# Gate and up: two of eight K tiles by a 2x2 block product with seven products

## The chip, the cores and the metric
The kernel runs on one core of one Trainium2 chip. The metric is the device time of one launch in microseconds (us). The engines are TensorE (PE; its weight loads are PEld), VectorE (DVE), ScalarE (ACT), GpSimd (POOL) and SyncE (SP, which here only issues DMAs).

## The reference
One layer of a hybrid encoder in float32, for 256 rows (S) of width 2048 (D), with a feed-forward width of 5632 (DFF). The part that the change touches is the feed-forward half and the final norm:

```
x = x + concat([hg_out, sb_out, mla_out]) @ w_o
h = rmsnorm(x, ffn_norm_g)
x = x + (silu(h @ w_gate) * (h @ w_up)) @ w_down
out = rmsnorm(x, final_norm_g)
```
w_gate and w_up are 2048 x 5632, w_down is 5632 x 2048. Ahead of it stand an RMSNorm, one input projection and three mixers (a gated linear recurrence, stick-breaking attention and latent attention), which the change leaves alone.

## The kernel before
**Products.** Every large product runs as three float32r matmuls. A tile is split into a part that float32r holds (`hi`, a ScalarE cast) and the rest (`lo`, a VectorE subtraction), and hi*hi + hi*lo + lo*hi is summed in one PSUM bank. The split of weights is in `split_w`: SP loads a raw slab of 256 rows by 512 columns (512 KB, [128, 2, 512] on the chip) into one of four `raw` slots, ScalarE casts it into one of four `hi` slots (L119), VectorE subtracts into one of four `lo` slots (through the helper at L91). `gemm_mm` (L151 to L153) then issues 12 matmuls of 512 columns for a slab: two blocks of 128 rows of x (b), two halves of the slab (j), three products. The stationary operand comes from x, already transposed and split (`at` tiles from the pool actp, 16 slots of 4 KB per partition; [128, hi/lo, j, 256]); the moving operand is the slab.

**Order.** The program is written in order and a planner (the Tile framework's list scheduler) fixes each engine's order before the run: of what is ready it takes what has the best priority, and priority follows the order of the text. The weight split stands in `tc.high_priority(offset=400)` (AHEAD), so it counts as 400 instructions earlier than where it is written. At run time each engine's queue is in order; a slot of a pool is reused when its last reader is done. Small side tasks (transposes of a finished tile, for example) are generators: `spawn` puts one in a list, and `tick`, called after each slab, runs one step of the first two.

**PSUM.** Eight banks: psA has four (`acc_tile` takes two, one for each block of rows), psM four (`bank`, for transposes and small products).

**Output projection.** Four groups of 512 columns of w_o, eight slabs each. `wo_end` (L791) adds the result to x (tiles x2[0..3] in the slots R0 to R3), takes the squares for the norm on ScalarE, and spawns `turn_x2`: TensorE transposes, then ScalarE and VectorE (`split_act`, L156 and L94) write the hi and lo of the transposed x times the norm's gain into an `at` tile. Eight such tiles, x2T[0..7], each 256 rows of the contraction over D, are the K tiles of gate and up.

**Gate and up.** For each of 11 groups of 512 columns `ff` runs the eight slabs of w_gate, then those of w_up (L845 to L854). Each has its own pair of banks. Silu with the row norm r2 is a ScalarE pass out of PSUM (L849), the product with up a VectorE pass. `turn_hid` then transposes the 512 hidden columns during the next slabs (L246) and splits them out of PSUM: hidden tiles 0 to 7 into `at` slots, 8 to 21 into `ht` slots of the pool `late`.

**Down projection and end.** Four passes of 22 slabs of w_down over the 22 hidden tiles; `settle` adds a pass to x2, `finish_rows` scales the rows by the final norm and stores them. In the last pass the last four slabs are run for one block of rows and then for the other. The gain of the final norm is one tile `gf`, loaded once.

Of the kernel before, what the change touches and what calls it, by code (L numbers as in the profile page):

```python
# [26 lines left out]
G_ATTN, G_FFN, G_HG, G_SB, G_MLA, G_QN, G_KVN, G_END = 0, 16, 32, 36, 42, 48, 52, 54  # L27
# [24 lines left out]
WIDTH = 2  # L52
SABBUFS = 3
WARM = 9
MAGIC = 12582912.0
LOGEXP = "natural_log_exp_and_others"


def build(tc, x, xT, pos, gains, fgain, lbraw, w_in, w_uq, w_ukv, w_o, w_gate, w_up, w_down, cst, msk, out, dbg=None):
    nc = tc.nc  # L60
    pe, act, dve, pool, sp = nc.tensor, nc.scalar, nc.vector, nc.gpsimd, nc.sync
    dbg = dbg or {}
    es = ExitStack()
# [39 lines left out]
    ahead = [0]  # L103

    def split_w(w, r0, c0, n, pieces=1, between=None):
        raw = slabp.tile([P, 2, 512], F32, name=nm("raw"), tag="raw", bufs=4)
        with tc.high_priority(offset=ahead[0]):
            hi = slabp.tile([P, 2, 512], F32R, name=nm("hi"), tag="hi")
            lo = slabp.tile([P, 2, 512], F32R, name=nm("lo"), tag="lo")
            at = ROWS[w.tensor.name] * c0 + r0 * n  # L110
            wv = w[at:at + 2 * P * n].rearrange("(p t c) -> p t c", p=P, t=2)
            for j in range(pieces):
                js = slice(j * 2 // pieces, (j + 1) * 2 // pieces)
                if between and j:
                    between(j)
                sp.dma_start(raw[:, js, :n], wv[:, js, :])
            for j in range(pieces):
                js = slice(j * 2 // pieces, (j + 1) * 2 // pieces)
                act.copy(hi[:, js, :n], raw[:, js, :n])  # L119
                tt(lo[:, js, :n], raw[:, js, :n], hi[:, js, :n].bitcast(F32), ALU.subtract)  # L120
        return hi, lo

    def gemm_slab(acc, w, r0, c0, n, at, start, stop, pieces=1, between=None):
        gemm_mm(acc, split_w(w, r0, c0, n, pieces, between), n, at, start, stop)
        tick()

    tasks = []
    spawn = tasks.append

    def tick():  # L130
        for t in tasks[:WIDTH]:
            if next(t, tasks) is tasks:
                tasks.remove(t)
# [5 lines left out]
    def flush():  # L139
        while tasks:  # L140
            tick()
# [40 lines left out]
    def gc(base, i):  # L182
        return gcol[:, base + i:base + i + 1]
# [102 lines left out]
    def rt(i):  # L286
        return resid.tile([P, 2, 512], F32, name=nm("R"), tag=f"R{i}")
# [501 lines left out]
    late = es.enter_context(tc.tile_pool(name="late", bufs=2))  # L789

    def wo_end(a, g):  # L791
        t = x2[g]
        for b in range(2):
            tt(t[:, b, :], t[:, b, :], a[b], ALU.add)
            junk = late.tile([P, 512], F32, name=nm("junk"), tag="junk", bufs=1)
            act.activation(junk, t[:, b, :], AF.Square, accum_out=ss2[:, 2 * g + b:2 * g + b + 1])

        def turn_x2():
            yield
            for i in range(2):  # L800
                ps = transpose4([[t[:, b, (2 * i + j) * P:(2 * i + j + 1) * P] for b in range(2)] for j in range(2)])
                at = act_tile()
# [20 lines left out]
    r2 = rsqrt_mean(ssum, D, 2)  # L823


    hid = {}

    def ff(w, c0):
        a = acc_tile()
        for i in range(8):  # L830
            gemm_slab(a, w, i * 256, c0, 512, x2T[i], i == 0, i == 7)
        return a

    def turn_hid(g, hh):
        yield
        for i in range(2):
            ps = transpose4([[hh[:, b, (2 * i + j) * P:(2 * i + j + 1) * P] for b in range(2)] for j in range(2)])
            n = 2 * g + i
            at = act_tile() if n < 8 else late.tile([P, 2, 2, 256], F32R, name=nm("ht"), tag="ht", bufs=14)
            pv = ps.rearrange("p (j n) -> p j n", j=2)  # L840
            act.copy(at[:, 0, :, :], pv)
            tt(at[:, 1, :, :], pv, at[:, 0, :, :].bitcast(F32), ALU.subtract)
            hid[n] = at

    for g in range(11):  # L845
        a = ff(w_gate, g * 512)
        sg = late.tile([P, 2, 512], F32, name=nm("sg"), tag="sg", bufs=1)
        for b in range(2):
            act.activation(sg[:, b, :], a[b], AF.Silu, scale=r2[:, b:b + 1])  # L849
        a = ff(w_up, g * 512)  # L850
        hh = late.tile([P, 2, 512], F32, name=nm("hh"), tag="hh", bufs=1)
        for b in range(2):
            stt(hh[:, b, :], a[b], r2[:, b:b + 1], sg[:, b, :], ALU.mult, ALU.mult)
        spawn(turn_hid(g, hh))  # L854

    gf = late.tile([P, D], F32, name="gf", bufs=1)
    sp.dma_start(gf, fgain.partition_broadcast(P))
    ss3 = sm(10, "ss3", 1)

    def settle(g, b, a, cs, col):  # L860
        tb = x2[g][:, b, cs]
        tt(tb, tb, a[b][:, cs], ALU.add)
        junk = late.tile([P, 512], F32, name=nm("junk"), tag="junk", bufs=1)
        act.activation(junk[:, cs], tb, AF.Square, accum_out=ss3[:, 5 * b + col:5 * b + col + 1])

    def finish_rows(b, cols):
        ssum = sm(1)
        dve.tensor_reduce(ssum, ss3[:, 5 * b:5 * b + cols], axis=AX.X, op=ALU.add)
        r3 = rsqrt_mean(ssum, D, 1)
        for k in range(4):  # L870
            o = x2[k][:, b, :]
            if k in (0, 2):
                act.activation(o, o, AF.Copy, scale=r3)
            elif k == 3:
                stt(o, o, r3, gf[:, k * 512:], ALU.mult, ALU.mult)
            else:
                ts(o, o, r3, ALU.mult)
            sp.dma_start(out[b * P:(b + 1) * P, k * 512:(k + 1) * 512], o)

    whole, left, right = slice(0, 512), slice(0, 256), slice(256, 512)  # L880
    for g in range(4):
        a = acc_tile()
        held = 4 if g == 3 else 0
        for k in range(22 - held):
            gemm_slab(a, w_down, k * 256, g * 512, 512, hid[k], k == 0, k == 21)
        if not held:
            for b in range(2):
                settle(g, b, a, whole, g)
                tb = x2[g][:, b, :]
                tt(tb, tb, gf[:, g * 512:(g + 1) * 512], ALU.mult)  # L890
# [79 lines left out]
```

## Time and profile before
| what | value |
|---|---|
| median of 3 runs | 1147.61 us (1147.3 to 1148.05) |
| profiled execution, its own time | 1148.17 us |
| its span in the trace | 1146.4 us |
| output projection, last group ends near | 407 us |
| gate and up, then down projection | 407 to 898 us, 898 to 1133 us |
| granted TensorE clock, mean | 0.998 |
| HBM traffic | 207.94 MB read, 2.10 MB written |

The profile is of one execution. "Busy" is the share of the span in which an engine executes; matmuls are pipelined, so the row of one matmul is longer than the distance between two starts. "Idle before, releaser" is the time an engine stood still ahead of an instruction and who ended that. The difference between an execution's own time and its span lies outside what the trace covers.

### The profile page before, as it was taken

To read this page: it belongs to the slowest core of one execution; us is meant where nothing else is said; L and a number is where in the kernel's file an instruction comes from. 1 tells how busy PE (TensorE), PEld (TensorE's weight loads), DVE (VectorE), ACT (ScalarE), POOL (GpSimd) and SP (SyncE) were. 2 spreads that over 40 slices of the span, in tenths; PEclk is the share of its full clock that TensorE was granted. 3 is DMA by queue.
4 is the path that set the end of the run, shared out by engine and by line. 5 is a ranking of instruction groups with operands and counts; after the bars stand their busy time and mean duration, and the time that the engine had idled before them with its cause. 6 is when DMAs were issued, how large, how long until landed. Compare 5 with 4: busy or idle time off the path is not lost.

```text
span 1146.4 us, 14162 instructions
## 1 busy us (share of the span) xinstructions
PE 1132.0 (99%) x5429; PEld 955.0 (83%) x5429; DVE 618.7 (54%) x703; ACT 546.7 (48%) x712; POOL 76.4 (7%) x110
## 2 busy tenths in 40 slices
PE   8999999999999999999999999999999999999997
PEld 4888899999988888888888888888888888888886
DVE  7798565455556555454454454454554545454543
ACT  7665565566645454444444444444444434343433
POOL 3196000011100000000000000000000000000000
PEclk9999999999999999999999999999999999999999
DMA  7745465544765656566666666666665666666662
GB/s 260 242 144 168 126 180 176 155 132 140 220 211 181 189 191 188 190 191 189 189 190 191 188 189 191 186 189 193 187 198 184 185 191 194 185 194 190 186 195 97
DMA packets 72004, 210.97 MB, mean 184 GB/s; under 512 B 7296, under 2 KB 24448, under 8 KB 71808
## 3 DMA queue, kind: packets, MB, share of 16 engines
q1 hardware_dynamic: 71936, 210.07, 58.8%
q8 instruction: 42, 0.69, 0.2%
q14 instruction: 26, 0.21, 0.1%
HBM read 207.94 MB, written 2.10 MB: 183 GB/s over the span
## 4 chain that ended last, share of the span: by engine, by line
PE 94%; DMA 1%; issue 1%; DVE 1%; ACT 1%; POOL 0%; SPq 0%; ACTq 0%; POOLq 0%; DVEq 0%
PE acc L152 29%; PE acc L153 29%; PE acc L151 29%; PE bank L246 2%; DVE lo L91 1%; PE bank L710 1%; PE bank L409 1%; DMA raw<-w_in 1%; PE acc L588 1%; PE acc L587 1%; PE acc L586 0%; PE bank L709 0%; ACT hi L119 0%; DMA L<-xT 0%; DMA sA<-pos 0%
## 5 line engine op out<-in xcount | busy, mean ns | idle before, releaser
L91 DVE TENSOR_TENSOR lo<-raw,hi 128x1024 fp32r<-128x1024 f32 (+3 forms) x410 | 480.9, 1175 | 480.6 <-ACT hi L119 480.2
L119 ACT CAST hi<-raw 128x1024 fp32r<-128x1024 f32 (+3 forms) x410 | 408.3, 998 | 529.0 <-PE acc L153 516.8
L151 PE MATMUL acc<-hi,at 128*128 128x512 f32 (+2 forms) x1352 | 517.0, 384 | 0.4 <-ACT hi L119 0.4
L152 PE MATMUL acc<-lo,at 128*128 128x512 f32 (+2 forms) x1352 | 513.9, 380 | 3.0 <-DVE lo L91 2.9
L153 PE MATMUL acc<-hi,at 128*128 128x512 f32 (+2 forms) x1352 | 512.8, 380 | 0.0
L152 PEld LDWEIGHTS acc<-lo,at 128*128 128x128 f32 x1352 | 254.1, 188 | 49.9 <-DVE lo L91 7.5
L151 PEld LDWEIGHTS acc<-hi,at 128*128 128x128 f32 x1352 | 253.9, 188 | 45.7 <-ACT hi L119 2.0
L153 PEld LDWEIGHTS acc<-hi,at 128*128 128x128 f32 x1352 | 253.8, 188 | 43.3
L152 PE MATMUL acc<-lo,ht 128*128 128x512 f32 (+1 forms) x232 | 89.8, 387 | 0.0
L151 PE MATMUL acc<-hi,ht 128*128 128x512 f32 (+1 forms) x232 | 89.8, 387 | 0.0
L153 PE MATMUL acc<-hi,ht 128*128 128x512 f32 (+1 forms) x232 | 89.8, 387 | 0.0
L175 POOL TENSOR_TENSOR sm<-sm,expo 128x4 f32<-128x4 f32 (+2 forms) x14 | 12.0, 857 | 911.3 <-DVE sm L100 911.3
L152 PEld LDWEIGHTS acc<-lo,ht 128*128 128x128 f32 x232 | 43.5, 187 | 10.0
L153 PEld LDWEIGHTS acc<-hi,ht 128*128 128x128 f32 x232 | 43.5, 187 | 9.9
L151 PEld LDWEIGHTS acc<-hi,ht 128*128 128x128 f32 x232 | 43.5, 187 | 9.9
L156 ACT ACTIVATE at<-bank,gcol 128x256 fp32r<-128x256 f32 x38 | 16.7, 470 | 10.5 <-DVE at L94 10.5
L94 DVE SCALAR_TENSOR_TENSOR at<-bank,gcol,at 128x256 fp32r<-128x256 f32 x38 | 17.2, 478 | 4.0 <-ACT at L156 4.0
L849 ACT ACTIVATE sg<-acc,sm 128x512 f32<-128x512 f32 x22 | 15.1, 685 | 3.1 <-PE acc L153 3.1
L94 DVE SCALAR_TENSOR_TENSOR hh<-acc,sm,sg 128x512 f32<-128x512 f32 x22 | 15.4, 743 | 0.0
L160 POOL TENSOR_TENSOR sA<-sA,sA 128x64 f32<-128x64 f32 x19 | 14.1, 745 | 1.2
L166 POOL TENSOR_SCALAR sA<-sA 128x64 f32<-128x64 f32 (+1 forms) x20 | 14.0, 698 | 1.7
L588 PE MATMUL acc<-at,lo 128*128 128x256 f32 x48 | 13.6, 284 | 0.0
(193 smaller groups left out, 501.3 us busy)
## 6 DMA issues: line engine op xcount, KB each, us to landing
raw<-w_gate SPq DMA_DIRECT2D x88, 512.0 KB, 3.5
raw<-w_up SPq DMA_DIRECT2D x88, 512.0 KB, 3.5
raw<-w_down SPq DMA_DIRECT2D x88, 512.0 KB, 3.5
raw<-w_in SPq DMA_DIRECT2D x48, 384.0 KB, 3.6
raw<-w_in SPq DMA_DIRECT2D x32, 512.0 KB, 3.5
raw<-w_o SPq DMA_DIRECT2D x32, 512.0 KB, 3.6
raw<-w_in SPq DMA_DIRECT2D x16, 256.0 KB, 5.4
raw<-w_in SPq DMA_DIRECT2D x8, 320.0 KB, 3.4
```

The lines of the kernel that those rows point to most:

```text
L91: dve.tensor_tensor(o, a, b, op=op)
L94: dve.scalar_tensor_tensor(o, a, s, b, op0=op0, op1=op1)
L119: act.copy(hi[:, js, :n], raw[:, js, :n])
L151: pe.matmul(o, lhsT=ah, rhs=hi[:, j, cs], start=start and j == 0, stop=False)
L152: pe.matmul(o, lhsT=ah, rhs=lo[:, j, cs], start=False, stop=False)
L153: pe.matmul(o, lhsT=al, rhs=hi[:, j, cs], start=False, stop=stop and j == 1)
L156: act.activation(dst[:, 0, j, :], src, AF.Copy, scale=g)
L160: pool.tensor_tensor(o, a, b, op=op)
L166: pool.tensor_scalar(o, a, s1, s2, op0=op0, op1=op1)
L246: pe.transpose(ps[:, j * 256 + b * P: j * 256 + (b + 1) * P], s, K[:, K_ID:K_ID + P])
L588: pe.matmul(o, lhsT=lo[:, j, ws], rhs=at[:, 0, j, :], start=False, stop=(2 * i + j == last))
L849: act.activation(sg[:, b, :], a[b], AF.Silu, scale=r2[:, b:b + 1])
```

## The change
A K tile of gate and up together is a product of a 2x2 block matrix (two row blocks of x by two K halves) with a 2x2 block matrix (two K halves by gate and up). For the first two of the eight K tiles (FAST = 2) it is done with seven block products in place of eight (Winograd's form of Strassen's scheme); the other six stay as they were, 12 matmuls for gate and 12 for up.

- `turn_x2`: for K tiles 0 and 1 ScalarE copies the four blocks out of PSUM times the gain, VectorE makes four sums, and all eight forms are split into an `ah` and an `al` tile (two `at` slots instead of one). Each x2[g] is also stored to DRAM, from ScalarE's queue.
- `fast_weights`: gate and up slab of a K tile go into one tile W. VectorE makes four weight sums T (three instructions); then the splits: both halves of gate (a), four sums (hT, lT), one half of up (b). The a and b splits take `hi` and `lo` slots of the old pool, T, hT and lT (two of each) come from a new pool `ffp`.
- The order in a group: the four shared products (p1, p6, p7, p5) of both K tiles into the four psM banks, then the three unshared ones (c11, c21, c12) of both into psA banks, then the six plain K tiles on top of c11, c21, c12 and c22. The shared products are summed on VectorE (u1 to u4) and added to the four results at the group's end.
- The hidden tiles are kept in float32 after their transposes (in `at` slots, in R0 to R3 and in one ffp tile) and split in the first pass of the down projection: 0 to 17 into `at` slots, 18 to 21 into slots of tag T. x2 is loaded back in that pass. The gains are loaded in two pieces after it.
- actp has 18 slots, and the scratch that GpSimd's DMAs would use is 1 KB.

```diff
+RAWS = 4
+FAST = 2
...
-    actp = es.enter_context(tc.tile_pool(name="actp", bufs=16))
+    actp = es.enter_context(tc.tile_pool(name="actp", bufs=18))
...
+        kept = dram.tile([P, 2, 512], F32, name=nm("kept"), tag=f"kept{g}", bufs=1)
+        act.dma_start(kept, t)
+        x2kept.append(kept)
...
+                if n >= FAST:
+                    at = act_tile()
+                    for j in range(2):
+                        split_act(at, j, ps[:, j * 256:(j + 1) * 256], gc(G_FFN, 2 * n + j))
+                    x2T[n] = at
+                    continue
+                A = ffp.tile([P, 8, P], F32, name=nm("T"), tag="T")
                 for j in range(2):
-                    split_act(at, j, ps[:, j * 256:(j + 1) * 256], gc(G_FFN, 4 * g + 2 * i + j))
-                x2T[2 * g + i] = at
+                    act.activation(A[:, 2 * j:2 * j + 2, :], ps[:, j * 256:(j + 1) * 256].rearrange("p (b n) -> p b n", b=2),
+                                   AF.Copy, scale=gc(G_FFN, 2 * n + j))
+                tt(A[:, 4, :], A[:, 1, :], A[:, 3, :], ALU.add)
+                tt(A[:, 5, :], A[:, 4, :], A[:, 0, :], ALU.subtract)
+                tt(A[:, 6, :], A[:, 1, :], A[:, 0, :], ALU.subtract)
+                tt(A[:, 7, :], A[:, 2, :], A[:, 5, :], ALU.subtract)
+                ah = actp.tile([P, 8, P], F32R, name=nm("at"), tag="at")
+                al = actp.tile([P, 8, P], F32R, name=nm("at"), tag="at")
+                act.copy(ah, A)
+                tt(al, A, ah.bitcast(F32), ALU.subtract)
+                x2T[n] = (ah, al)
...
+    def halve(src, js, hi=None, lo=None):
+        hi = hi or slabp.tile([P, 2, 512], F32R, name=nm("hi"), tag="hi")
+        lo = lo or slabp.tile([P, 2, 512], F32R, name=nm("lo"), tag="lo")
+        act.copy(hi[:, js, :], src[:, js, :])
+        tt(lo[:, js, :], src[:, js, :], hi[:, js, :].bitcast(F32), ALU.subtract)
+        return hi, lo
+    def fast_weights(wa, wb, r0, c0):
+        with tc.high_priority(offset=ahead[0]):
+            W = ffp.tile([P, 4, 512], F32, name=nm("W"), tag="W")
+            for w, js in ((wb, slice(0, 2)), (wa, slice(2, 4))):
+                at = ROWS[w.tensor.name] * c0 + r0 * 512
+                sp.dma_start(W[:, js, :], w[at:at + 2 * P * 512].rearrange("(p t c) -> p t c", p=P, t=2))
+            T = ffp.tile([P, 4, 512], F32, name=nm("T"), tag="T")
+            tt(T[:, 0:2, :], W[:, 0:1, :].broadcast_to([P, 2, 512]), W[:, 1:3, :], ALU.subtract)
+            tt(T[:, 2, :], W[:, 1, :], T[:, 1, :], ALU.subtract)
+            tt(T[:, 3, :], W[:, 3, :], T[:, 2, :], ALU.subtract)
+            hT = ffp.tile([P, 4, 512], F32R, name=nm("hT"), tag="hT")
+            lT = ffp.tile([P, 4, 512], F32R, name=nm("lT"), tag="lT")
+            a = halve(W[:, 2:4, :], slice(0, 2))
+            halve(T, slice(0, 2), hT, lT)
+            halve(T, slice(2, 4), hT, lT)
+            b = halve(W[:, 0:2, :], slice(1, 2))
+        return a, b, (hT, lT)
+    ACROSS = (("p1", 0, 0, 0), ("p6", 5, 2, 2), ("p7", 6, 2, 0), ("p5", 4, 2, 1))
+    ALONE = (("c11", 2, 0, 1), ("c21", 3, 2, 3), ("c12", 7, 1, 1))
+    def fast_unit(accs, products, ws, forms, start):
+        ah, al = forms
+        for name, f, which, k in products:
+            hi, lo = ws[which]
+            o = accs[name]
+            last = name[0] == "p" and start == "last"
+            pe.matmul(o, lhsT=ah[:, f, :], rhs=hi[:, k, :], start=start is True, stop=False)
+            pe.matmul(o, lhsT=ah[:, f, :], rhs=lo[:, k, :], start=False, stop=False)
+            pe.matmul(o, lhsT=al[:, f, :], rhs=hi[:, k, :], start=False, stop=last)
...
+        for nme, b, (hi, lo) in (("c11", 0, wa), ("c21", 1, wa), ("c12", 0, wb), ("c22", 1, wb)):
+            o = accs[nme]
+            for j in range(2):
...
+        if g < 6:
+            f = actp.tile([P, 2, 512], F32, name=nm("at"), tag="at")
+        elif g < 10:
+            f = rt(g - 6)
+        else:
+            f = ffp.tile([P, 2, 512], F32, name=nm("hf"), tag="hf", bufs=1)
+        for i in range(2):
...
+    for g in range(11):
+        accs = {}
+        fast = [fast_weights(w_gate, w_up, i * 256, g * 512) for i in range(FAST)]
+        for n in ("p1", "p6", "p7", "p5"):
+            accs[n] = bank()
+        for i in range(FAST):
+            fast_unit(accs, ACROSS, fast[i], x2T[i], True if i == 0 else "last" if i == FAST - 1 else False)
+        for n in ("c11", "c21", "c12", "c22"):
+            accs[n] = acc1()
+        for i in range(FAST):
+            fast_unit(accs, ALONE, fast[i], x2T[i], i == 0)
+        u1, u3, u2, u4 = part("s1"), part("u3"), part("u2", 2), part("v", 2)
+        act.copy(u1, accs["p1"])
+        tt(u2, u1, accs["p6"], ALU.add)
+        tt(u3, u2, accs["p7"], ALU.add)
+        tt(u2, u2, accs["p5"], ALU.add)
+        tt(u4, u3, accs["p5"], ALU.add)
+        for i in range(FAST, 8):
+            with tc.high_priority(offset=ahead[0]):
+                wa = halve(load(w_gate, i * 256, g * 512), slice(0, 2))
+                wb = halve(load(w_up, i * 256, g * 512), slice(0, 2))
+            plain_unit(accs, wa, wb, x2T[i], i == FAST, i == 7)
+            if g == 0 and i == FAST:
+                flush()
+            tick()
+        for b, (ug, cg, uu, cu) in enumerate(((u1, "c11", u2, "c12"), (u3, "c21", u4, "c22"))):
+            tt(ug, ug, accs[cg], ALU.add)
+            act.activation(ug, ug, AF.Silu, scale=r2[:, b:b + 1])
+            tt(uu, uu, accs[cu], ALU.add)
+            stt(uu, uu, r2[:, b:b + 1], ug, ALU.mult, ALU.mult)
+        spawn(turn_hid(g, (u2, u4)))
...
+    def split_hid(n):
+        if n < 18:
+            at = act_tile()
+        else:
+            if n % 2 == 0:
+                pairs.append(ffp.tile([P, 2, 2, 2, 256], F32R, name=nm("T"), tag="T"))
+            at = pairs[-1][:, n % 2]
+        f = hidf[n].rearrange("p (j n) -> p j n", j=2)
+        act.copy(at[:, 0, :, :], f)
+        tt(at[:, 1, :, :], f, at[:, 0, :, :].bitcast(F32), ALU.subtract)
+        hid[n] = at
...
+            if g == 0:
+                with tc.high_priority(offset=ahead[0]):
+                    split_hid(k)
+                if k in (14, 16, 18, 20):
+                    i = (k - 14) // 2
+                    x2[i] = rt(i)
+                    sp.dma_start(x2[i], x2kept[i])
             gemm_slab(a, w_down, k * 256, g * 512, 512, hid[k], k == 0, k == 21)
+        if g == 0:
+            for i in range(2):
+                t = ffp.tile([P, 2, 512], F32, name=nm("hT"), tag="hT")
+                sp.dma_start(t, fgain[i * 1024:(i + 1) * 1024].partition_broadcast(P))
+                gf += [t[:, 0, :], t[:, 1, :]]
...
+    nc = bacc.Bacc("TRN2", target_bir_lowering=False, num_devices=1, dynamic_dma_scratch_size=1024)
```

## Rows read from the trace of the kernel before

**Rows 1.** The page: busy, shares and instructions; granted clock by slices; the chain by engine.
```profile
PE 1132.0 (99%) x5429; PEld 955.0 (83%) x5429; DVE 618.7 (54%) x703; ACT 546.7 (48%) x712; POOL 76.4 (7%) x110
...
PEclk9999999999999999999999999999999999999999
...
PE 94%; DMA 1%; issue 1%; DVE 1%; ACT 1%; POOL 0%; SPq 0%; ACTq 0%; POOLq 0%; DVEq 0%
```
**Rows 2.** Waits of TensorE, whole kernel: who for whom, us in total, times, longest.
```profile
PE acc L152 <- DVE lo L91: 2.9, 6, 0.8
```
**Rows 3.** Waits of all engines from 390 to 920 us.
```profile
ACT hi L119 <- PE acc L153: 294.2, 188, 1.8
DVE lo L91 <- ACT hi L119: 262.7, 190, 2.0
```
**Rows 4.** Chain in order of time, 586 to 634 us: start, us, what.
```profile
587.96 0.87 PE bank L246 x8
...
632.38 0.87 PE bank L246 x8
```
**Rows 5.** Timeline of TensorE in the down projection: start, us, engine, line, operation.
```profile
955.21 0.39 PE L151 MATMUL acc<-hi,at 128*128 128x512 f32 x1
...
976.97 0.39 PE L151 MATMUL acc<-hi,ht 128*128 128x512 f32 x1
...
1016.16 0.39 PE L151 MATMUL acc<-hi,at 128*128 128x512 f32 x1
```
**Rows 6.** Windows, one group: us; busy of each engine; clock, DMA share, GB/s.
```profile
632.38:676.81 44.43, 44.43 (x203) 36.88 (x201) 22.12 (x20) 19.11 (x20) 0.00 (x0) 1.00 0.61 190
```
**Rows 7.** Tile raw from 410 to 898 us: duration in ns, least, median, most.
```profile
L91 DVE TENSOR_TENSOR lo<-raw,hi x176: 1224/1225/1227, 411.4 to 897.3; 128x1024 fp32r<-128x1024 f32 x176
L116 SPq DMA_DIRECT2D raw<-w_up x88: 327/328/331, 409.9 to 874.1; - x88
```
**Rows 8.** Groups by shape: busy us, mean ns of one; idle before, releaser.
```profile
L119 ACT CAST hi<-raw 128x1024 fp32r<-128x1024 f32 x328 | 344.9, 1052 | 481.1 <-PE acc L153 473.8 <-issue 5.8 <-ACT hi L119 0.7
...
L94 DVE SCALAR_TENSOR_TENSOR at<-bank,gcol,at 128x256 fp32r<-128x256 f32 x38 | 17.2, 478 | 4.0 <-ACT at L156 4.0
...
L94 DVE SCALAR_TENSOR_TENSOR hh<-acc,sm,sg 128x512 f32<-128x512 f32 x22 | 15.4, 743 | 0.0
L849 ACT ACTIVATE sg<-acc,sm 128x512 f32<-128x512 f32 x22 | 15.1, 685 | 3.1 <-PE acc L153 3.1
...
L91 DVE TENSOR_TENSOR R<-R,acc 128x512 f32<-128x512 f32 x15 | 9.7, 681 | 3.3 <-PE acc L153 3.3
L119 ACT CAST hi<-raw 128x512 fp32r<-128x512 f32 x16 | 9.6, 608 | 0.5 <-DMA raw<-w_in 0.5
...
L91 DVE TENSOR_TENSOR R<-L 128x512 f32<-128x512 f32 x13 | 9.3, 741 | 0.0
...
L841 ACT CAST ht<-bank 128x512 fp32r<-128x512 f32 x14 | 7.5, 583 | 0.0
```
**Rows 9.** Timeline of ScalarE within a group; in brackets idle before and releaser.
```profile
594.34 1.05 ACT L119 CAST hi<-raw 128x1024 fp32r<-128x1024 f32 x1 [1.67 <-PE acc L153]
```
**Rows 10.** Timeline of VectorE in the same group.
```profile
595.43 1.23 DVE L91 TENSOR_TENSOR lo<-raw,hi 128x1024 fp32r<-128x1024 f32 x1 [1.49 <-ACT hi L119]
...
625.35 1.22 DVE L91 TENSOR_TENSOR lo<-raw,hi 128x1024 fp32r<-128x1024 f32 x1 [1.49 <-ACT hi L119]
626.49 1.40 DVE L94 SCALAR_TENSOR_TENSOR hh<-acc,sm,sg 128x512 f32<-128x512 f32 x2
628.07 1.22 DVE L91 TENSOR_TENSOR lo<-raw,hi 128x1024 fp32r<-128x1024 f32 x1 [0.18 <-ACT hi L119]
```
**Rows 11.** The page: DMA issues, KB each, median us from issue to landing.
```profile
raw<-w_gate SPq DMA_DIRECT2D x88, 512.0 KB, 3.5
```
**Rows 12.** Windows, the tail.
```profile
1133.00:1146.40 13.40, 5.25 (x46) 5.05 (x44) 4.38 (x12) 4.42 (x10) 1.10 (x2) 0.87 0.46 157
```
**Rows 13.** Timeline of TensorE in the opening.
```profile
14.62 0.50 PE L152 MATMUL acc<-lo,at 128*128 128x512 f32 x1 [0.82 <-DVE lo L91]
```
**Rows 14.** Windows around that wait.
```profile
12.00:16.00 4.00, 3.05 (x12) 2.21 (x13) 4.00 (x6) 4.00 (x9) 2.35 (x2) 1.00 1.06 399
```

More of the change, by code (lines that the diff above doesn't have):

```diff
@@ L105, in split_w @@
     def split_w(w, r0, c0, n, pieces=1, between=None):
-        raw = slabp.tile([P, 2, 512], F32, name=nm("raw"), tag="raw", bufs=4)
+        raw = slabp.tile([P, 2, 512], F32, name=nm("raw"), tag="raw", bufs=RAWS)
         with tc.high_priority(offset=ahead[0]):
@@ L788, in build @@
     mix.__exit__(None, None, None)
-    late = es.enter_context(tc.tile_pool(name="late", bufs=2))
+    dram = es.enter_context(tc.tile_pool(name="dram", bufs=1, space=bass.MemoryType.DRAM))
+    x2kept = []
+    ffp = es.enter_context(tc.tile_pool(name="ffp", bufs=2))
     def wo_end(a, g):
@@ L794, in wo_end @@
             tt(t[:, b, :], t[:, b, :], a[b], ALU.add)
-            junk = late.tile([P, 512], F32, name=nm("junk"), tag="junk", bufs=1)
+            junk = ffp.tile([P, 512], F32, name=nm("s1"), tag="s1", bufs=1)
             act.activation(junk, t[:, b, :], AF.Square, accum_out=ss2[:, 2 * g + b:2 * g + b + 1])
+        kept = dram.tile([P, 2, 512], F32, name=nm("kept"), tag=f"kept{g}", bufs=1)
+        act.dma_start(kept, t)
+        x2kept.append(kept)
         def turn_x2():
@@ L823, in build @@
     r2 = rsqrt_mean(ssum, D, 2)
-    hid = {}
[L828 to L856, printed above, removed]
@@ L857, in build, with acc1, load @@
-    sp.dma_start(gf, fgain.partition_broadcast(P))
+    def acc1():
+        return psA.tile([P, 512], F32, name=nm("acc"), tag="acc")
+    def load(w, r0, c0):
+        raw = slabp.tile([P, 2, 512], F32, name=nm("raw"), tag="raw", bufs=RAWS)
+        at = ROWS[w.tensor.name] * c0 + r0 * 512
+        sp.dma_start(raw, w[at:at + 2 * P * 512].rearrange("(p t c) -> p t c", p=P, t=2))
+        return raw
+    def halve(src, js, hi=None, lo=None):
[4 more added lines that the diff above has]
+        return hi, lo
@@ new lines, in fast_weights @@
+    def fast_weights(wa, wb, r0, c0):
+        with tc.high_priority(offset=ahead[0]):
+            W = ffp.tile([P, 4, 512], F32, name=nm("W"), tag="W")
+            for w, js in ((wb, slice(0, 2)), (wa, slice(2, 4))):
+                at = ROWS[w.tensor.name] * c0 + r0 * 512
+                sp.dma_start(W[:, js, :], w[at:at + 2 * P * 512].rearrange("(p t c) -> p t c", p=P, t=2))
[10 more added lines that the diff above has]
+        return a, b, (hT, lT)
@@ new lines, in plain_unit @@
+    def plain_unit(accs, wa, wb, at, start, stop):
+        for nme, b, (hi, lo) in (("c11", 0, wa), ("c21", 1, wa), ("c12", 0, wb), ("c22", 1, wb)):
+            o = accs[nme]
+            for j in range(2):
+                ah = at[:, 0, j, b * P:(b + 1) * P]
+                al = at[:, 1, j, b * P:(b + 1) * P]
+                pe.matmul(o, lhsT=ah, rhs=hi[:, j, :], start=start and nme == "c22" and j == 0, stop=False)
+                pe.matmul(o, lhsT=ah, rhs=lo[:, j, :], start=False, stop=False)
+                pe.matmul(o, lhsT=al, rhs=hi[:, j, :], start=False, stop=stop and j == 1)
@@ new lines, in part, with turn_hid @@
+    def part(tag, bufs=1):
+        return ffp.tile([P, 512], F32, name=nm(tag), tag=tag, bufs=bufs)
+    def turn_hid(g, hs):
+        if g < 6:
[5 more added lines that the diff above has]
+        for i in range(2):
+            ps = transpose4([[hs[b][:, (2 * i + j) * P:(2 * i + j + 1) * P] for b in range(2)] for j in range(2)])
+            act.copy(f[:, i, :], ps)
+            hidf[2 * g + i] = f[:, i, :]
+            yield
@@ new lines, in build @@
+    hidf = {}
+    for g in range(11):
[29 more added lines that the diff above has]
+        spawn(turn_hid(g, (u2, u4)))
@@ L858, in build @@
+    hid = {}
+    pairs = []
+    def split_hid(n):
[9 more added lines that the diff above has]
+        hid[n] = at
     ss3 = sm(10, "ss3", 1)
@@ L862, in settle @@
         tt(tb, tb, a[b][:, cs], ALU.add)
-        junk = late.tile([P, 512], F32, name=nm("junk"), tag="junk", bufs=1)
+        junk = ffp.tile([P, 512], F32, name=nm("s1"), tag="s1", bufs=1)
         act.activation(junk[:, cs], tb, AF.Square, accum_out=ss3[:, 5 * b + col:5 * b + col + 1])
@@ L874, in finish_rows @@
             elif k == 3:
-                stt(o, o, r3, gf[:, k * 512:], ALU.mult, ALU.mult)
+                stt(o, o, r3, gf[k], ALU.mult, ALU.mult)
             else:
@@ L878, in finish_rows @@
             sp.dma_start(out[b * P:(b + 1) * P, k * 512:(k + 1) * 512], o)
+    gf = []
     whole, left, right = slice(0, 512), slice(0, 256), slice(256, 512)
@@ L889, in build @@
                 tb = x2[g][:, b, :]
-                tt(tb, tb, gf[:, g * 512:(g + 1) * 512], ALU.mult)
+                tt(tb, tb, gf[g], ALU.mult)
             continue
@@ L962 @@
     arrays = arrays_of(inputs)
-    nc = bacc.Bacc("TRN2", target_bir_lowering=False, num_devices=1)
+    nc = bacc.Bacc("TRN2", target_bir_lowering=False, num_devices=1, dynamic_dma_scratch_size=1024)
     aps = {n: nc.dram_tensor(n, a.shape, mybir.dt.from_np(a.dtype), kind="ExternalInput").ap() for n, a in arrays.items()}
```

2 lines of the change are left out of this document (1 added, 1 removed).

## Prediction
> **What bounds the kernel now.** I read the busy shares first: TensorE is busy for 99% of the span, VectorE for 54%, ScalarE for 48%, and the granted clock is 9 in tenths (full) in every slice [rows 1]. A busy share alone doesn't prove a bound, so the chain that ended last comes next: 94% of it is TensorE, VectorE 1%, DMA 1% [rows 1]. Then the waits: over the whole kernel TensorE's longest entry is 2.9 us, for lo halves [rows 2]; in the stretch of gate and up it is the others who wait, ScalarE 294 us for TensorE and VectorE 263 us for ScalarE, and TensorE has no entry [rows 3]. So there time is the number of matmuls times their pitch. The chain between two groups gives the period: transposes at 587.96 and at 632.38, 44.42 us [rows 4]. In it are 16 slabs of 12 matmuls and 8 transposes (0.87 us), so (44.42 - 0.87)/192 = 0.2268 us a matmul. The reader should see that this is far under the 0.39 us that a matmul's own row shows; the pitch of starts counts. In the down projection it differs: eight slabs whose stationary tile is `at` take 976.97 - 955.21 = 21.76 us for 96 matmuls, 0.2267 each; the 14 slabs with `ht` take 1016.16 - 976.97 = 39.19 us for 168, 0.2333 each [rows 5].
>
> **The change, part by part.** Sums are made against the profiled execution, 1148.17 us (span 1146.4 and 1.77 outside it); the median of the three runs is 0.56 lower, and I carry differences over to it.
>
> *Removed matmuls.* A K tile of 256 rows of gate and of up takes 8 block products of 3 matmuls, 24; with seven products it is 21. Two tiles in 11 groups: 11 x 2 x 3 = 66 matmuls at 0.2267, **-14.96 us**.
>
> The starts of these matmuls of 512 columns are 227 or 233 ns apart [rows 5]. The Trainium skill, page "TensorE: Matmul & The Clock Gate", section "Back-to-back issue gap", gives 215.7 ns for an isolated stream of this width and 131 ns for a sustained one. By these figures, as estimates, the term would be 14.2 or 8.6 us; the measurement decides.
>
> *The hidden tiles' new place.* For tiles 8 to 17 the halves now go into `at` slots instead of `ht`: 10 slabs x 12 x 4 passes = 480 matmuls. If the pitch follows the pool, each gains 0.0066 us, 3.2 us; if it follows something else, 0. The slabs `hi` and `lo` are the same in all of [rows 5] and only the stationary tile differs, so I take **-3.2**.
>
> *Moving tiles from the new pool.* Four of seven products read hT and lT: 4 x 3 x 2 x 11 = 264 matmuls. No row has a moving slab outside its old pool; by the nearest, the two pitches 0.0066 us apart, it is between -1.7 and +1.7 us. I take half of the upper end, **+0.9**, since the only tile of a late pool that the trace shows was the slower one.
>
> *VectorE in a group.* Before, 22.1 us of 44.4 [rows 6]. After: 12 plain lo halves x 1.225 = 14.7 [rows 7]. For each fast tile one 1024-wide sum (1.225, as the lo halves of the same width), two of 512 from SBUF (0.741 each), and 3.5 lo halves (3 x 1.225 + 0.741): 7.1, twice 14.2. Four sums with a PSUM input at 0.681 = 2.7. The end of the group: four more at 0.681 and two products at 0.743 = 4.2. Together 35.9 us in a group of 186 x 0.2267 + 0.87 = 43.0: 83% [rows 7, 8]. ScalarE: 12 + 7 hi halves of 1.05, the copy out of PSUM and two more at 0.583, two Silu of 0.685, some 23 us, 54% [rows 8]. Neither is the bound as a total; what counts is lateness.
>
> *The tightest wait.* The four slots of hi and lo are a rolling lead: in the rows a hi cast starts when TensorE frees a slot, 1.05 us, and the lo half ends 2.32 us after that start (594.34 to 596.66) [rows 9, 10], while the lead is three slabs, 36 matmuls, 8.2 us. In the new order the two gate and two up halves of both fast tiles hold all four slots until the unshared products. The first is free at matmul 27 of the 42, and the first plain slab needs it at 42: 15 x 0.2267 = 3.40 us against 2.32. **Slack 1.1 us**, the least of the group; the next slab has 21 matmuls, 4.8 us, then 30 and 36. Around it VectorE has the next groups' three sums (2.7) and the four sums out of PSUM (2.7). Its queue is in order, so what stands ahead decides: nothing or one short sum, no loss; one 1.225 us sum just begun, 0.15; all seven, 5.4 - 1.1 = 4.3 us. How the planner's order comes out can be seen: the group's two products (626.49) fill a gap between lo halves, the next of which starts at its usual distance of 2.72 us [rows 10], and TensorE waits for no lo half there [rows 3]. That is near the lower end; I take 0.2 a group, **+2.2**.
>
> *Banks.* All eight are in use. The four of the shared products are complete at matmul 24 and wanted next by the transposes behind matmul 66, 9.5 us later. The four of the sums are single: c11 is complete 18 matmuls before the group's end and wanted 24 after its start, 9.5 us for one 0.68 us sum; c22 is complete at the end and wanted after 42 + 18 matmuls, 13.6 us. Nothing, while VectorE is not 5 us behind. At the start of the down projection the cover shrinks: its second accumulator wants c21's bank 18 matmuls (4.1 us) after that is complete, between 0 and 1 us once, **+0.3**.
>
> *Loads.* The fast tiles' four slabs are the same four 512 KB transfers on SP; they go into W, which is free again once the up half of its last content is split, about a group (43 us) before the next use, against 3.5 us to landing [rows 11]. x2 goes out (four issues on ScalarE's queue, behind which stand its hi casts; an issue on SP takes 0.33 us [rows 7]) and comes back on SP's queue, 4 MB in all, beside a DMA share of 0.61 [rows 6]; it is read again 8 slabs (22 us) after its load at the earliest. Nothing; if that cover were gone, four landings, 14 us. The gains move to two loads two passes ahead of use: nothing. All slabs are issued on SP [rows 11] and none of the new transfers on POOL, so POOL's smaller scratch costs nothing.
>
> *Forms of x for the two fast tiles, and the second split of the hidden tiles.* The first cost ScalarE one cast of 1.05 more a tile, and VectorE 1.225 and four sums of 128 columns, each at most the 0.478 of 256 [rows 8], in place of two of 0.478: up to 2.2 more. They are made in the output projection, over 15 slabs (41 us) before use: nothing; uncovered, 3.3 a tile. The second adds a 0.608 cast and a 0.741 half to each of 22 slabs of the first down pass: VectorE 1.97, ScalarE 1.66 of 2.72 us, with the lead of 8.2 us and the first tiles free earlier: nothing; without that cover one chain of 1.35 us. The tail after 1133 us is the same code [rows 12].
>
> **Sum:** -14.96 - 3.2 + 0.9 + 2.2 + 0.3 = -14.8. 1148.17 - 14.8 = 1133.4; on the median **1132.8**. Its own range goes from no lateness and no dearer moving tile (-18.2, 1129.4) to no gain in the down projection, hT at the slow pitch and 0.4 us a group (+3.2 + 0.8 + 2.2): 1139.
>
> **Rivals.** (1) *One long VectorE sum in the way in every group.* The slack is as thin as one operation, and 83% leaves little room after a mistimed order. 1.225 us instead of 0.2, 11 times: +11.3, 1144. Against it: VectorE is idle for 1.5 us before nearly every lo half now [rows 10].
> (2) *Slower: the first plain slab behind the whole batch.* Place: that slab's lo half, queued behind the next tile's three sums and the four sums out of PSUM. 4.3 us x 11 = 47 in place of the 2.2: 1178. It decides from (14.96 + 3.2 - 0.9 - 0.3)/11 = 1.5 us a group. For it: an in-order queue and no trace of these operations; against it: the lo halves of the slabs are planned ahead of other work, and 4.3 us would have to recur in each group.
> (3) *The change doesn't bring the down projection's gain, the pitch being tied to something else:* 1136, inside the first case's range.
> (4) *The clock falls.* If TensorE pauses at every turn of banks and its clock went to 1.2 GHz for the 42 matmuls after it, 9.5 us a group, +105: 1238. Against it: in the opening TensorE paused 0.82 us for a lo half, and the granted clock of that stretch stayed 1.00 (2.4 GHz) [rows 13, 14]. The same page, section "A second HAM failure mode: psum-queue depth-cycling", tells of a kernel that cycled through its PSUM banks and had its clock go up and down; rows 13 and 14 speak against it here.
>
> **How the numbers follow.** The forecast with its range 0.70 (rival 3 in it), rival 1 0.15, rival 2 0.12, rival 4 0.02, 0.01 left. The range leaves out a thin lower end (0.05) and rivals 2 and 4: 1129.5 to 1144.5. Under 0.2% (2.3 us), about what a measurement of this kernel can tell from no change, lie parts of rival 1 and of small versions of rival 2: 0.05. Faster 0.82, slower 0.13.
>
> **What would show it.** Group period 43.1 us between transposes; TensorE's wait for lo halves under 5 us over the 11 groups, at the first plain slab if anywhere; VectorE 36 us a group; a pitch of 0.2267 in the down projection up to tile 17, and 0.233 for the last four; the tail as before. Wrong is the forecast if the period stays at 44.4 or more, or if the matmuls with hT start over 0.24 us apart.

## The result, and the profile after

The changed kernel takes 1133.24 us, the median of four runs (1132.23 to 1134.29), against 1147.63 of the kernel before in the same session: a ratio of 0.9875, 95% interval 0.9857 to 0.9892. The prediction was 1132.8. The profiled execution took 1133.12 us with a span of 1131.4, 15.0 under the 1146.4 of before.

The page of the changed kernel: span, busy shares, granted clock, chain that ended last, and the loads of W (KB each, median us to landing).

```profile
span 1131.4 us, 14321 instructions
PE 1117.2 (99%) x5363; PEld 941.7 (83%) x5363; DVE 758.4 (67%) x907; ACT 595.2 (53%) x791; POOL 76.4 (7%) x110
PEclk9999999999999999999999999999999999999999
PE 93%; DMA 2%; DVE 2%; issue 2%; ACT 1%; SPq 0%; POOL 0%; ACTq 0%; POOLq 0%; DVEq 0%
...
W<-w_gate SPq DMA_DIRECT2D x22, 512.0 KB, 4.6
```

Beside [rows 1] TensorE is as busy as before with fewer matmuls, VectorE went from 54 to 67%, and the chain is still TensorE's. Next, what TensorE waited for (us in total, times, longest):

```profile
PE acc L154 <- DVE lo L93: 2.9, 6, 0.8
...
PE acc L906 <- DVE lo L93: 0.3, 1, 0.3
```

The first, and three entries left out here (1.4, 0.9 and 0.3 us), lie ahead of gate and up; the last is the only one in it, 0.3 us in 11 groups. So the time there is again a count of matmuls times a pitch. The period, from the chain (start us, us, what):

```profile
506.40 0.44 PE bank L248 x4
...
549.68 0.44 PE bank L248 x4
...
766.08 0.44 PE bank L248 x4
...
809.94 0.44 PE bank L248 x4
```

It is 43.28 us where [rows 4] had 44.42, and once 43.86 (766.08 to 809.94). The window of one group, to be held against [rows 6] (us, busy time and count of PE, PEld, DVE, ACT and POOL, clock, DMA share, GB/s):

```profile
506.40:549.68 43.28, 43.28 (x196) 35.69 (x195) 33.41 (x37) 22.24 (x25) 0.00 (x0) 1.00 0.60 196
```

By stage, from first matmul to first matmul (the table of the kernel before puts its borders some us later, near 407 and 898): up to gate and up 404.7 us before and 404.3 after (-0.3); gate and up 488.7 and 476.9 (-11.8); down projection and end 253.1 and 250.2 (-2.9). The sum is -15.0. The borders, first of before and then of after (TensorE, start us, us of one):

```profile
404.66 0.39 PE L151 MATMUL acc<-hi,at 128*128 128x512 f32 x1
...
893.34 0.39 PE L151 MATMUL acc<-hi,at 128*128 128x512 f32 x1
```
```profile
404.32 0.39 PE L895 MATMUL bank<-hi,at 128*128 128x512 f32 x1
...
881.19 0.39 PE L153 MATMUL acc<-hi,at 128*128 128x512 f32 x1
```

The last stage wasn't where seven products are used at all; that part came with the tiles' new places, which the timeline of the changed kernel shows:

```profile
929.69 0.39 PE L155 MATMUL acc<-hi,at 128*128 128x512 f32 x1
...
931.05 0.40 PE L155 MATMUL acc<-hi,at 128*128 128x512 f32 x1
931.28 0.39 PE L153 MATMUL acc<-hi,T 128*128 128x512 f32 x1
...
931.98 0.40 PE L153 MATMUL acc<-hi,T 128*128 128x512 f32 x1
```

From 929.69 to 931.05 six starts take 1.36 us, 0.2267 each; from 931.28 to 931.98 three take 0.70, 0.2333 each. All hidden tiles in `at` now run at the fast pitch of [rows 5], the four left in T slots at the slow one, and a later pass takes 60.16 us in place of 60.96: 216 x 0.2267 + 48 x 0.2333 = 60.2. The four passes, the tail counted with the last, are 0.58, 0.80, 0.80 and 0.71 us shorter.

### The profile page after: what moved, and what is told of

Same layout as the page of the kernel before. It is cut to its first block, busy times and chain, and to the rows that moved or that the text cites. A ratio compares the mean times of both kernels' runs of the same rounds, so it can differ in the third digit from the quotient of the medians.

```text
span 1131.4 us, 14321 instructions
## 1 busy us (share of the span) xinstructions
PE 1117.2 (99%) x5363; PEld 941.7 (83%) x5363; DVE 758.4 (67%) x907; ACT 595.2 (53%) x791; POOL 76.4 (7%) x110
## 4 chain that ended last, share of the span: by engine, by line
PE 93%; DMA 2%; DVE 2%; issue 2%; ACT 1%; SPq 0%; POOL 0%; ACTq 0%; POOLq 0%; DVEq 0%
PE acc L153 15%; PE acc L155 15%; PE acc L154 15%; PE acc L906 10%; PE acc L907 10%; PE acc L905 10%; PE bank L248 2%; PE bank L895 2%; PE bank L896 2%; PE bank L897 2%; PE acc L895 1%; PE acc L896 1%; PE acc L897 1%; DVE lo L93 1%; PE bank L712 1%
## 5 line engine op out<-in xcount | busy, mean ns | idle before, releaser
L93 DVE TENSOR_TENSOR lo<-raw,hi 128x1024 fp32r<-128x1024 f32 (+3 forms) x366 | 424.3, 1167 | 279.3 <-ACT hi L121 217.7
L121 ACT CAST hi<-raw 128x1024 fp32r<-128x1024 f32 (+3 forms) x234 | 223.0, 956 | 246.2 <-PE acc L155 224.2
L154 PE MATMUL acc<-lo,at 128*128 128x512 f32 (+2 forms) x808 | 302.4, 374 | 3.1 <-DVE lo L93 2.9
L153 PE MATMUL acc<-hi,at 128*128 128x512 f32 (+2 forms) x808 | 304.4, 379 | 0.0
L155 PE MATMUL acc<-hi,at 128*128 128x512 f32 (+2 forms) x808 | 301.3, 373 | 0.0
L905 PE MATMUL acc<-hi,at 128*128 128x512 f32 x528 | 207.5, 393 | 0.0
L906 PE MATMUL acc<-lo,at 128*128 128x512 f32 x528 | 205.6, 389 | 0.3 <-DVE lo L93 0.3
L907 PE MATMUL acc<-hi,at 128*128 128x512 f32 x528 | 205.7, 390 | 0.0
L862 ACT CAST hi<-raw 128x1024 fp32r<-128x1024 f32 x132 | 136.6, 1051 | 130.0 <-PE acc L907 97.2
L93 DVE TENSOR_TENSOR lo<-W,hi 128x1024 fp32r<-128x1024 f32 (+1 forms) x44 | 42.0, 956 | 34.6 <-ACT hi L862 34.6
L93 DVE TENSOR_TENSOR lT<-T,hT 128x1024 fp32r<-128x1024 f32 x44 | 52.6, 1216 | 0.0
L862 ACT CAST hT<-T 128x1024 fp32r<-128x1024 f32 x44 | 45.1, 1046 | 0.5 <-DVE T L93 0.4
```

Of the source, the lines that this page charges most:

```text
L153: pe.matmul(o, lhsT=ah, rhs=hi[:, j, cs], start=start and j == 0, stop=False)
L154: pe.matmul(o, lhsT=ah, rhs=lo[:, j, cs], start=False, stop=False)
L155: pe.matmul(o, lhsT=al, rhs=hi[:, j, cs], start=False, stop=stop and j == 1)
L862: act.copy(hi[:, js, :], src[:, js, :])
L905: pe.matmul(o, lhsT=ah, rhs=hi[:, j, :], start=start and nme == "c22" and j == 0, stop=False)
L906: pe.matmul(o, lhsT=ah, rhs=lo[:, j, :], start=False, stop=False)
```

## The experiments

**What sets the pitch: the pool, or where a tile starts?** By the order of the pools and the sizes of their tiles (each rounded up to 32 bytes), every tile of `raw`, `hi`, `lo` and `at` starts 32 bytes past a multiple of 64 within its partition; the `ht` tiles of before and the tiles of the new pool `ffp` start at a multiple of 64. No trace shows an address. A pad of 32 bytes ahead of a pool moves what follows it by half of 64. Theory A: the pitch is 0.2333 us where the stationary and the moving tile start at different places within 64 bytes, and 0.2267 where they agree. B: it goes with the pool. C: a start at 32 bytes is fast, one at 0 slow. Three kernels: the pad ahead of `ffp` in the changed kernel, ahead of `late` in the kernel before, and ahead of all large pools in the changed one (which moves `ffp` to 32 and all the others to 0).

```diff
     pool.memset(expo, -0.5)
+    pad = small.tile([P, 8], F32, name="pad", tag="pad", bufs=1)
+    pool.memset(pad, 0.0)
```

(The third has the pad in the pool `cons` instead.) Expected of the first, the second and the third:

> The changed kernel with an unused tile of 32 bytes per partition ahead of the new pool ffp, so that its tiles start 32 bytes past a multiple of 64, as hi, lo and the at tiles do; before that they start at a multiple of 64. Theory A (the pitch depends on whether stationary and moving tile start at the same place within 64 bytes): the 264 matmuls with hT and lT and the 192 with the last four hidden tiles go from 0.2333 to 0.2267 us, 456 x 0.0066 = 3.0 us less, a span of 1128.4. Theory B (the pitch belongs to the pool or to high addresses): no difference, 1131.4.

> The kernel before with the same 32 bytes ahead of its pool late. Theory A: the slabs with ht run at 0.2267, 14 x 12 x 4 = 672 matmuls x 0.0066 = 4.4 us less, a span of 1142.0. Theory B: no difference, 1146.4.

> The changed kernel with the 32 bytes ahead of all large pools: hi, lo and at now start at multiples of 64, ffp 32 bytes past. Theory A (only the relation of the two counts): no difference, span 1131.4. Theory C (an operand at a multiple of 64 is slow whatever the other is): the some 4,300 float32r matmuls of 512 columns on hi, lo and at tiles go to 0.2333, 28 us more, 1159. Theory B: no difference.

Measured: 1130.32 us, ratio to the kernel before 0.9846 (0.9831 to 0.9860); 1143.60, ratio 0.9960 (0.9946 to 0.9974), 4.3 under the kernel before it; 1134.03, ratio 0.9880 (0.9865 to 0.9895). The tile views show why. The duration of one matmul's row goes with its pitch: 389 ns at 0.2267, 394 to 396 at 0.2333 (columns: line, engine, operation and tiles, count; min/median/max ns; first and last start). In turn the changed kernel, the first, the third (its `hT`, then its slabs in gate and up), the kernel before, and the kernel before with its pad:

```profile
L895 PE MATMUL bank<-hT,at x66: 395/396/397, 405.0 to 842.8; 128*128 128x512 f32 x66
```
```profile
L897 PE MATMUL bank<-hT,at x66: 389/389/389, 405.5 to 841.2; 128*128 128x512 f32 x66
```
```profile
L897 PE MATMUL bank<-hT,at x66: 395/396/397, 404.6 to 842.2; 128*128 128x512 f32 x66
...
L907 PE MATMUL acc<-hi,at x480: 388/389/474, 456.9 to 880.0; 128*128 128x512 f32 x160
```
```profile
L151 PE MATMUL acc<-hi,ht x232: 277/394/397, 916.0 to 1137.7; 128*128 128x512 f32 x108, 128*128 128x256 f32 x8
```
```profile
L151 PE MATMUL acc<-hi,ht x232: 278/389/390, 919.0 to 1136.6; 128*128 128x512 f32 x108, 128*128 128x256 f32 x8
```

The same pool is slow or fast by its start, so B falls. With everything else at 0 and `ffp` at 32, the matmuls of `hT` with `at` are slow as before while those of the slabs keep their pace, so C falls: only the relation of the two starts counts. Nothing but 0 and 32 was tried, and why it is so stays open.

**Do the two sets of transposes cost?** The changed `turn_hid` transposes in two sets of four, where [rows 4] has one chain of eight. This kernel makes one set.

```diff
     for i in range(2):
...
         hidf[2 * g + i] = f[:, i, :]
-        yield
+    yield
```

> The changed kernel with the eight transposes of a hidden group in one step of the side task instead of four in each of two. Theory: each set of transposes costs its own time and a dearer restart of the stream of matmuls (0.31 us in place of 0.23 to the next start); in the before kernel a set of eight costs 0.90 us, in the changed one two sets of four 1.03. One set: 0.13 x 11 = 1.4 us less, a span of 1130.0. Rival: the two sets cost nothing of their own and the difference lies elsewhere in the group: no difference, 1131.4.

Measured: 1133.61 us, ratio 0.9872 (0.9858 to 0.9887). The period in its chain:

```profile
506.05 0.87 PE bank L248 x8
549.31 0.87 PE bank L248 x8
```

43.25 or 43.26 instead of 43.28: the theory falls, two sets cost 0.02 to 0.03 us a group. This kernel too had one late group (43.71 us).

**How much lateness of VectorE can the order bear?** Four and six idle sums of 1024 columns are added for each fast tile, at the place of the real ones.

```diff
     def fast_weights(...):
+            for _ in range(4):          # 6 in the second
+                tt(T[:, 2:4, :], W[:, 0:1, :].broadcast_to([P, 2, 512]),
+                   W[:, 1:3, :], ALU.subtract)
```

> The changed kernel with eight more VectorE sums of 1024 columns a group (four for each fast tile, into a half of T that is overwritten after them), 1.13 us from start to start when they follow each other: VectorE 33.4 + 9.0 = 42.4 of a period of 43.3 us. Theory: lateness is set by the order, in which the planner keeps the first plain slabs' lo halves ahead of what can wait, so TensorE waits under 1 us a group and the span stays under 1142. Rival 2 of the prediction: the sums stand ahead of the first plain slab's lo half, which ends 1.1 us before its use now, so four or more of them cost 3.4 us a group and over: 1169 and more.

> The same with twelve more sums a group: VectorE 33.4 + 13.6 = 47.0 us. Both theories: VectorE becomes the bound, the period of a group goes to 47 us or more, 11 x 3.7 = 41 us more: a span of 1172 or more. A period under 46 would say that busy time is not what bounds VectorE.

With four: 1145.02 us, ratio 0.9978 (0.9967 to 0.9989), 11.8 over the changed kernel. Its two longest waits, and windows of one group and of a stretch near 450:

```profile
PE bank L248 <- DVE R L93: 5.0, 1, 5.0
PE acc L909 <- DVE at L96: 3.0, 1, 3.0
```
```profile
518.36:561.64 43.28, 43.28 (x197) 35.69 (x195) 42.54 (x46) 22.26 (x25) 0.00 (x0) 1.00 0.62 201
...
450.00:453.00 3.00, 3.00 (x8) 2.34 (x7) 0.02 (x1) 0.96 (x1) 0.00 (x0) 0.50 0.01 3
```

In the group shown VectorE is busy 42.5 of 43.28 us, 98% (in the next 42.0), and from 518 us on the period hasn't moved by 0.01. The loss is two single waits where the first groups' sums collide with the turn of x2, 8.0 us, and behind each three to four us of matmuls at half the clock. So neither theory had the place; and rival 2 of the prediction, a batch in the way in every group, falls with eight more sums in it.

With six, a single run: 1243.39 us. Its longest wait in total, and windows:

```profile
PE bank L248 <- ACT s L940: 57.2, 4, 15.2
```
```profile
531.00:546.50 15.50, 0.34 (x3) 0.02 (x2) 14.98 (x17) 3.78 (x5) 0.00 (x0) 0.59 0.11 34
546.50:550.50 4.00, 4.00 (x10) 3.22 (x11) 3.93 (x6) 2.66 (x3) 0.00 (x0) 0.50 0.00 0
```

VectorE's work in a group, 47.0 us as reckoned, is now more than TensorE's 43.28, and the kernel doesn't get slower by the excess alone: TensorE stands still for 14 to 15 us every other group, comes back at clock 0.50, and two groups take 108 us where 2 x 47.0 is 94. The wait is the one that the prediction's paragraph on the banks left out on the condition that VectorE is not 5 us behind: the transposes wait for a bank, and ScalarE's copy of p1 out of it waits for VectorE.

**Does the order of the fast tiles matter?** Shared and unshared products of one tile, then of the other.

```diff
         for i in range(FAST):
+            fast_unit(accs, ACROSS, fast[i], x2T[i], ...)
             fast_unit(accs, ALONE, fast[i], x2T[i], ...)
```

(The loop that ran ACROSS for both tiles first goes.)

> The changed kernel with all seven products of one fast tile before those of the other, instead of the shared products of both first. The first hi/lo slots come free at matmul 15 in place of 27, so the first plain slab's lead grows from 15 to 27 matmuls (6.1 us); c11 is wanted 12 matmuls (2.7 us) after the group's start in place of 24. Theory: neither wait is reached in either order, no difference, span 1131.4 within 0.5. Rival: the order of the products is what keeps TensorE from waiting for the banks of the last group, whose sums end some 0.5 us after the group's start: up to 1 us a group, 1142.

Measured: 1132.67 us, ratio 0.9863 (0.9848 to 0.9877), every period 43.28, no late group: no difference that can be told, as the theory had it.

**Is the gain the count of matmuls?** Three matmuls are added to each fast tile.

```diff
+            (ah, al), (hi, lo) = x2T[i], fast[i][0]
+            for l, r in ((ah, hi), (ah, lo), (al, hi)):
+                pe.matmul(accs["c12"], lhsT=l[:, 0, :], rhs=r[:, 0, :],
+                          start=False, stop=False)
```

> The changed kernel with three matmuls more for each fast tile (x's first form times gate's first half, added into the bank of c12, so that result is not what it should be): 192 matmuls a group as before, all else as in the changed kernel. Theory: the gain is the count of matmuls, so the period goes from 43.28 to 43.28 + 6 x 0.2267 = 44.64 and the span to 1146.4. Rival: part of the gain comes from elsewhere in gate and up (fewer passes, other order), then the span stays below 1144.

Measured: 1148.15 us, ratio 1.0000 (0.9990 to 1.0009); all of the change is there but the count, and nothing is left of its gain. The chain's period is 44.64 (in two groups 0.1 to 0.2 more), 1.36 over 43.28, which is 6 x 0.2267:

```profile
555.26 0.44 PE bank L248 x4
...
599.90 0.44 PE bank L248 x4
```

That nothing at all is left is a meeting of two other terms. The down projection keeps its gain (250.2 us, 2.9 under before), and gate and up take 491.3 us, 2.6 more than before with the same count; 1.7 of it is the pitch of `hT`.

**More tiles.** With the pad, one set of transposes and the tiles in turn (two tiles), and with the pad and the tiles in turn for three and four tiles:

```diff
-FAST = 2
+FAST = 3          # and 4
```

> Two fast tiles, tile by tile, with the new pool 32 bytes further and the eight transposes in one step: the edits of e1, e4 and e7 together. They touch different terms, so they add: 1128.7 (e1) less 0.3 (e4's period 43.25 for 43.28) less 0.6 (e7 has no late group): a span of 1127.8. Rival: they don't add, 1128.7 or more.

> The same two shifts of order and pool (tile by tile, 32 bytes), transposes in two steps, and three fast tiles instead of two. Three matmuls fewer a group and tile: 11 x 3 x 0.2267 = 7.5 us less than two tiles, a span near 1120.8. VectorE goes from 33.4 to some 37.4 of 42.4 us a group, under the 42.4 of 43.3 that e5 carried without a wait in the later groups. hT and lT have two slots for three tiles: the third tile's are free at matmul 21 and needed at 45, 5.4 us for a chain of 3.3. Theory: no wait, 1120.8. Rival: that chain stands behind the sums of the group's turn, 1 to 2 us a group: 1132 to 1143.

> As e10 with four fast tiles. Counted by matmuls a further 7.5 us, 1113.3, with VectorE at 33.4 + 8 = 41.4 of 41.8 us. Theory: the share alone would still be carried, but the third and fourth tile need 6.3 us of VectorE each within the 4.8 us that a fast tile's 21 matmuls last, with two slots of T, hT and lT, so TensorE waits some 1 to 3 us a group: 1124 to 1146. Rival: carried, 1113 to 1116.

Measured, the three in one session: 1129.70 us, ratio 0.9838 (0.9816 to 0.9861), with nothing to be told from the pad alone (three spans of 1127.9 to 1128.0 and one of 1132.2); 1122.43, ratio 0.9765 (0.9747 to 0.9782); 1125.01, ratio 0.9789 (0.9772 to 0.9806). Three tiles beat both kernels: the chain's shares and a group of theirs are

```profile
PE 96%; issue 1%; DVE 1%; ACT 1%; DMA 0%; SPq 0%; ACTq 0%; POOLq 0%; POOL 0%; DVEq 0%
```
```profile
509.45:551.89 42.44, 42.44 (x193) 35.14 (x192) 37.17 (x42) 23.41 (x28) 0.00 (x0) 1.00 0.60 198
```

and with four tiles, with a stretch of the chain,

```profile
PE 64%; DVE 21%; DMA 8%; issue 5%; ACT 1%; SPq 1%; ACTq 0%; POOLq 0%; POOL 0%; DVEq 0%
```
```profile
573.29 4.47 DMA W<-w_gate
...
577.86 1.22 DVE T L93
...
582.67 1.22 DVE lT L93
583.89 1.14 DVE T L93
585.02 1.13 DVE lT L93
...
589.54 5.63 DMA W<-w_gate
```

The third tile takes 0.67 us more out of the period of the padded kernel (43.11 to 42.44), its three matmuls. The fourth gives nothing on the whole: gate and up take 469.4 us against 467.0 with three, where the count alone would take 7.5 us off. The four periods from 473.90 to 643.22 lie between 41.83, which is the count's 41.8, and 42.65, with 42.33 in the mean; the longest waits stand in other groups (us in total, times, longest):

```profile
PE acc L909 <- DVE at L96: 2.2, 1, 2.2
PE bank L898 <- DVE lT L93: 1.4, 1, 1.4
```

The first is the turn of x2 again, the second an `lT` half; five groups more have stops of some 0.1 us for an `lT` half. In the stretch of the chain shown it has left TensorE: it goes round from a W load to the sums and halves of VectorE (busy 40.9 us of the 42.33 from 600.89 to 643.22, 97%) to the next W load. That 98% of VectorE did no harm with the idle sums and 97% does with four tiles fits with this chain: the idle sums had no reader, these have, and the loads wait for them. No run separates that from other causes.

## Why the prediction was right

**Removed matmuls, -14.96.** Right, and shown by itself: with the 66 put back the median is 14.9 us over the changed kernel's (the medians of the kernel before differ by 0.7 between these two sessions), and the period grows by 1.36 us, 6 x 0.2267. The estimates of 14.2 and 8.6 us by the Trainium skill's page "TensorE: Matmul & The Clock Gate", section "Back-to-back issue gap", don't fit; 0.2267 us a matmul does. By those estimates the period would have grown by 1.29 or 0.79.

**Hidden tiles, -3.2, and start of the down projection, +0.3.** Together -2.9, and -2.9 measured: 0.80 in each of the two middle passes, less in the first and the last. The cause was put as "the pitch follows the pool"; it is the relation of the tiles' starts, and the prediction's size came out because `at` tiles start where the slabs do. So rival 3 had its condition, something other than the pool, and not its price.

**Moving tiles from the new pool, +0.9.** Mis-sized: the matmuls with `hT` and `lT` start 0.2333 apart, as `ht` did, so 264 x 0.0066 = 1.74 us, the upper end of the range given. The rows of the changed kernel, nine starts from the first shown to the last:

```profile
448.49 0.40 PE L895 MATMUL bank<-hT,at 128*128 128x512 f32 x1
...
450.59 0.40 PE L895 MATMUL bank<-hi,at 128*128 128x512 f32 x1
```

2.10 us for nine. The padded kernel takes this away, and that of the last four hidden tiles (192 x 0.0066 = 1.27): 3.0 reckoned, 2.9 measured.

**VectorE's lateness, +2.2.** Mis-sized the other way: 0.6 us, in one group, and 0 in the ten others. Of the tightest place the prediction had the slack right. Between the transposes at 506.40 and 549.68 the next group begins, and its first plain slab's lo half is wanted by that slab's second matmul, at 544.30. VectorE's queue there, and that matmul:

```profile
538.99 0.68 DVE L93 TENSOR_TENSOR T<-W,T 128x512 f32<-128x512 f32 x1
539.59 0.67 DVE L93 TENSOR_TENSOR u<-s,bank 128x512 f32<-128x512 f32 x1
...
540.98 1.22 DVE L93 TENSOR_TENSOR T<-W 128x1024 f32<-128x1024 f32 x1
542.11 1.22 DVE L93 TENSOR_TENSOR lo<-raw,hi 128x1024 fp32r<-128x1024 f32 x1
```
```profile
544.30 0.39 PE L906 MATMUL acc<-lo,at 128*128 128x512 f32 x1
```

It ends at 543.33, 1.0 us early, though sums of the batch do stand right ahead of it: the order puts them there early enough. The lateness came from the paragraph on loads, which put them at nothing. It counted about a group (43 us) from W's freeing to its next use, but the next use is not a matmul: it is VectorE's sum `T<-W` of the next group, which the order puts right behind the load. For the sum at 540.98 the load was issued here:

```profile
536.40 0.43 SPq L872 DMA_DIRECT2D W<-w_gate  x1
```

That is 4.6 us ahead, and 4.6 is the median to landing: by the trace it landed 0.1 us before the sum, and 0.1 to 0.3 before it in the other steady groups. One landed later, and the sum that waited for it stood at the head of the queue with the first plain lo half behind it. The chain of the late group:

```profile
796.09 5.81 DMA W<-w_gate
...
803.13 1.23 DVE lo L93
...
804.41 0.50 PE acc L906
```

That is the place of rival 2, once and for 0.6 us: the sum started 5.9 us after its load was issued instead of 4.6, 1.0 of that was covered by the slack, and TensorE waited 0.3 and started again more slowly.

**Gate and up together:** -14.96 + 0.9 + 2.2 = -11.86 forecast, -11.8 measured. The period came out at 43.28 and not at 43.1: 0.16 of it is the pitch of `hT`. What is left, 0.8 us over the 11 groups, had no term. In a steady group it is 0.06 us (1.14 measured against 1.36 - 0.16); the two sets of transposes explain 0.02 to 0.03 of it, and the rest stays open. That the stage agrees to 0.1 us is luck: the errors of the two terms, +0.8 for the pitch of `hT` and -1.6 for lateness, and the 0.8 without a term cancel. The -0.3 ahead of gate and up had no term, and is less than the runs of one kernel differ by (1147.3 to 1148.05 before).

**VectorE, 36 us a group:** 33.4. The rows' durations overlap: two sums in a row start 0.60 or 1.13 us apart, where their rows show 0.68 and 1.22. A sum of rows overstates an engine that runs back to back.

**Rivals 1, 2 and 4.** 1144 falls: there is no wait of that kind in each group. 1178 falls even with eight sums more. The granted clock stayed at 1.00 in gate and up, where TensorE has one wait of 0.3 us, so 1238 falls; that it can fall to 0.50 behind waits is seen in the kernels with idle sums.

## What to carry to other kernels

Where TensorE is the bound and nothing waits, a cut in the count of matmuls was worth its count times the pitch, until the work that it puts on another engine closed a loop with the loads of its operands; look for that loop in the chain, not in the busy share alone (three tiles at 88% VectorE gain in full, the fourth at 97% loses, and idle sums at 98% cost nothing in the steady groups). Look at the pitch by tile: the same matmul at two pitches is a question of where the two tiles start, and 32 bytes of padding were worth 2.9 and 4.3 us here. Where a new operation's slack is worked out from rows, the lead of its load belongs in the sum as much as the queue ahead of it, and that lead runs to the first reader in the order, which may be a sum long ahead of the matmul.

## What the runs showed of the hardware

Matmuls of 512 columns start 226.7 ns apart when the stationary and the moving tile start at the same place within 64 bytes (both 32 or both 0), and 233.3 when one starts at 0 and the other at 32.

After a pause of TensorE of 3.0 us (eight more sums) its granted clock was 0.50 (1.2 GHz) in the stretch 450 to 453 and matmuls started 0.43 us apart; in the stretch 454 to 456 it was 1.00 (2.4 GHz) again. After the pause of 0.82 us of [rows 13] it had stayed at 1.00, and so it did from 440 to 446 after the pause of 2.2 us with four tiles. With twelve more sums it was 0.50 from 528 to 530, behind two pauses of 1.2 us each, which ended at 525.48 and 527.42.

Two VectorE sums of float32 that follow each other start 0.60 us (512 columns) or 1.13 us (1024 columns) apart, where one's own row shows 0.68 and 1.22.
